# Latent attention of a hybrid decoder layer: scores two units ahead of their transposes, queries and keys loaded apart from values, shorter filling steps

## The chip, the cores and the metric

The kernel runs on one core of a Trainium2 chip. The metric is the time of the whole kernel on the device, in microseconds (us). Below, PE is TensorE (matrix products and transposes), ACT is ScalarE, DVE is VectorE, POOL is GpSimd, SP is SyncE; SP and POOL also issue the kernel's loads and stores, each in the order of its own queue.

## The reference, cut to what matters

```
h = x + 0.5 * swiglu(rms_norm(x), ffn1)
proj = rms_norm(h) @ w_in          # c_q, c_kv, k_rope, sb_qkv, gates
q, k, v = latent projections of c_q and c_kv, 8 heads: 96 for q and k, 64 for v
o_mla = softmax(mask(q k^T / sqrt(96))) v          # per head, S = 1024
o_sb  = stick_breaking(sq, sk, sv)                 # per head, 8 heads of 64
g_mla, g_sb = split(sigmoid(gates))
merged = g_mla * (o_mla @ w_branch_mla) + g_sb * (o_sb @ w_branch_sb)
h = h + merged @ w_out
h = h + 0.5 * swiglu(rms_norm(h), ffn2)
h = h + sigmoid(rms_norm(h) @ w_ple_gate) * (p @ w_ple_proj)
```

All of it is float32. SEQ is 1024, D_MODEL is 1024, each SwiGLU has 2816 hidden columns.

## The kernel before

**Arithmetic.** A float32 product is made of three matmuls: each operand is split into a rounded upper part (HI) and the rest (LO), and `mm3` (L180 holds the matmul itself) adds HI·HI, HI·LO and LO·HI. The split takes a cast on ACT (L139 for weights, L210 and L261 for results) and a subtraction on POOL or DVE (L140, L211, L262).

**Order.** The order of PE's instructions is the order in which the program writes them. The order on the other engines and on the queues of SP and POOL comes out of a scheduler that simulates the program; each engine and each queue then works strictly in that order.

**Attention.** The loop near the end of the attention phase runs over `units`, triples (m, head, un). m is 0 for stick-breaking and 1 for the latent attention (MLA). The queries of a head come in four chunks of 256 (two tiles of 128 each), and chunk c sees 256·(c+1) keys. Unit un = 0 holds chunks 0 and 1, unit 1 chunk 2, unit 2 chunk 3; in steps of 256 keys that makes 3, 3 and 4 steps, ten for a head. One step writes, in this order:

- transposes of a block of the probabilities (`tr`, L184: 3 or 4 matmuls of 128 columns into a bank `T`; ACT casts the bank to `pt` HI at L210, DVE makes LO at L211);
- the scores of a later unit, as far as `todo` has them (`A<-hd`; 128 queries against all their keys into a tile `A`, of which there are two, then the mask);
- the product of the block that was transposed two steps before with the values (`accum`, `T<-pt,hv`, 4 matmuls of 256 or 128 columns), and at the end of a chunk copies on ACT (L1124, L1129), an addition on DVE (L1130) and a split on ACT and POOL into `oT` (L1137, L1138);
- matmuls that belong to other work, up to the time `goal` of the program's own count (`fill`). During MLA this work is the output branch of stick-breaking, `branches_sb`: 192 matmuls of 512 columns in all, which show as `T<-oT,D`. Its results go over ACT (`bt`, L824), POOL (L825) and SP to the DRAM tensor `msb_d` (L826).

The softmax of an MLA tile is a maximum on DVE (L1200), an exponential on ACT (L1202), a reciprocal and a scaling on DVE (L1203, L1204); the result (`p` for chunks 0 and 1, a tile `D` of the weights' pool for chunks 2 and 3) is what a later step transposes.

Loads of a head come from POOL's queue into 9 tiles with the tag `hd`: queries HI and LO, keys HI and LO, values (`hv`).

**After attention.** `merge_up` makes the gated sum of both branches, one column tile `ct` of 128 at a time: 24 matmuls on `oT` (`T<-oT,D`), a multiplication by the gate and an addition of `msb` on DVE, and a split into `hid`. Two column tiles share one load of gates and one of `msb_d`: into `D` tiles for ct 0 and 1, into `gm` tiles for each later pair. The `gm` tiles are taken from the pool `u` and so from the memory of `o_t[1]`, the stick-breaking outputs that `branches_sb` reads. With two column tiles at hand `down_chunk` adds their product with `w_out` to h (`T<-D,hid`, 96 matmuls); for this the stream is read again from `h_spill` into `h2`, in memory that attention gives back, and two rows of `w_out` are loaded and split per chunk (the first two are called dw0 and dw1 below, tiles D_12961 and D_12966). PE writes ct 0, 1 and 2 ahead of the first down chunk (72 matmuls). All these loads are in SP's queue.

Of the kernel before, what the change touches and what calls it, by code (L numbers as in the profile page):

```python
# [27 lines left out]
H = 8  # L28
# [18 lines left out]
def hybrid_layer_kernel(  # L47
# [73 lines left out]
    v_d = dram.tile([H, S, P], F32, name="v_d")  # L121
# [579 lines left out]
    for c in range(2):  # L701
        col = slice(c * 512, (c + 1) * 512)
        for t in range(NT):
# [7 lines left out]
            n = c * NT + t  # L711
# [68 lines left out]
    def branch_w(w, ct):  # L780
        d = load_split([(0, w[:, ct * P:(ct + 1) * P].rearrange("(k q) c -> q k c", q=P))], 512)
        return d[:, :, :512].rearrange("q l (k c) -> q l k c", k=4)
# [26 lines left out]
    def branches_sb(first):  # L809

        nxt = first
        for ct in range(KT):
            d = nxt
            if ct + 1 < KT:
                nxt = branch_w(w_branch_sb, ct + 1)
            gt = load_row(gate_d, KT + ct)
            bt = rawp.tile([P, 1024], F32, tag="raw", name="bt")
            for half in range(2):
                tk = slice(half * 512, (half + 1) * 512)
                ps = bank()  # L820
                for k in range(4):
                    mm3(ps, d[:, HI, k], d[:, LO, k], o_t[1][HI][:, k, tk], o_t[1][LO][:, k, tk], k == 0, k == 3)
                    yield
                nc.scalar.copy(bt[:, tk], ps)  # L824
                nc.gpsimd.tensor_mul(bt[:, tk], bt[:, tk], gt[:, tk])  # L825
            nc.sync.dma_start(out=msb_d[ct], in_=bt)  # L826
# [6 lines left out]
    def fill(ns):  # L833
        t0 = pe["t"]
        while pe["t"] < t0 + ns:
            if next(filler[0], filler) is filler:
                break
        left[0] -= pe["t"] - t0
# [297 lines left out]
    def split_o(dst, pair, op, cs):  # L1136
        nc.scalar.copy(dst[HI][:, pair, cs], op[:, cs])  # L1137
        nc.gpsimd.tensor_sub(dst[LO][:, pair, cs], op[:, cs], dst[HI][:, pair, cs].bitcast(F32))  # L1138
# [7 lines left out]
    def load_rows(src):  # L1146
        r = ap.tile([P, S], F32R, tag="hd", name="hd", bufs=9)
        for p0, rows in src:
            nc.gpsimd.dma_start(out=r[p0:p0 + rows.shape[0]], in_=rows)
        return r  # L1150

    def load_v(src, head):
        vt = ap.tile([P, NT, P], F32R, tag="hd", name="hv", bufs=9)
        nc.gpsimd.dma_start(out=vt, in_=src[head].rearrange("(k q) c -> q k c", q=P))
        return vt
# [26 lines left out]
        return be  # L1182

    def mla_load(head):
        q = [load_rows([(0, q_d[head, :, l, :])]) for l in range(2)]
        k = [load_rows([(0, k_d[head, :, l, :])]) for l in range(2)]
        return q, k, None, load_v(v_d, head)

    def mla_products(hd, i, ps):
        q, k, _, _ = hd  # L1190
# [18 lines left out]
    units = [(m, hd, un) for m in range(2) for hd in range(H) for un in range(3)]  # L1209
# [3 lines left out]
    def head_of(m, hd):  # L1213
        if (m, hd) not in loaded and hd < H:
            loaded[m, hd] = (mla_load if m else sb_load)(hd)
        return loaded.get((m, hd))

    def scores(m, hd, idx):

        ch = idx[0] // 2  # L1220
        if (m, hd, ch) not in shared:
            shared[m, hd, ch] = [ptile(256 * (ch + 1)) for _ in range(2 - m)]
        one = acc_tile() if ch < 2 else None
        pss = [one[:, 512 * (i % 2):512 * (i % 2) + 512] if ch < 2 else acc_tile() for i in idx]
        for i, ps in zip(idx, pss):
            (mla_products if m else sb_products)(head_of(m, hd), i, ps)
        for i, ps in zip(idx, pss):
            probs[m, hd, i] = (mla_probs if m else sb_probs)(i, ps, shared[m, hd, ch])

    def start_mla():  # L1230
        first = branch_w(w_branch_sb, 0)
        fill(1e9)
        for b in range(2):
            o_t.append([upool.tile([P, 4, S], F32R, tag="u", name="oT") for _ in range(2)])
        for j in range(4):
            split_o(o_t[1], j, pairs[j], slice(0, S))
        filler[0] = branches_sb(first)
        left[0] = KT * 24 * 216.0
# [4 lines left out]
        scores(0, 0, (2 * c, 2 * c + 1))  # L1243
    fill(5500.0)
    queue = []

    def run_av():
        pt, ac = queue.pop(0)
        ac(pt)

    for n, (m, hd, un) in enumerate(units):
        if (m, hd, un) == (1, 0, 0):
            while queue:
                run_av()
            start_mla()
        todo = []
        if n + 1 < len(units):
            m2, hd2, un2 = units[n + 1]
            todo = []
            for c in unit_ch[un2]:  # L1260
                both = (2 * c, 2 * c + 1)
                todo += [(m2, hd2, ix) for ix in ([both] if m2 or c < 2 else [both[:1], both[1:]])]
        if un == 1:
            head_of(m, hd + 1) if hd + 1 < H else head_of(m + 1, 0) if m == 0 else None
        steps = []
        for c in unit_ch[un]:
            steps += av_steps(hd, c, [probs.pop((m, hd, 2 * c + a)) for a in range(2)], head_of(m, hd)[3], m == 1)
        for k, (tr, ac) in enumerate(steps):
            t0 = pe["t"]
            take = -(-len(todo) // (len(steps) - k))  # L1270
            pt = tr()
            for x_ in todo[:take]:
                scores(*x_)
            todo = todo[take:]
            queue.append((pt, ac))
            if len(queue) > 2:
                run_av()
            goal = (2500.0, 1600.0)[m]
            if m == 0 or left[0] > 0 or (hd == H - 1 and un > 0):
                fill(t0 + goal - pe["t"])  # L1280
    while queue:
# [146 lines left out]
```

## Time and profile before

| | us |
|---|---|
| time, median of 3 runs | 2365.31 (2364.64 to 2365.52) |
| the profiled execution, own time | 2360.41 |
| its span in the profile | 2358.3 |
| PE busy | 2292.8 (97%) |
| DVE, ACT, POOL busy | 1543.9, 980.4, 751.1 |
| granted TensorE clock, mean over the span | 0.991 of full speed |

The span runs from the first to the last instruction of one execution; that execution's own time is 2.1 us more than its span and 4.9 us less than the median of the runs. MLA runs from 1277.5 us (first score maximum of its first head) to 1470.9 us (first matmul of the merge).

### The profile page before, as it was taken

To read this page: it belongs to the slowest core of one execution; us is meant where nothing else is said; L and a number is where in the kernel's file an instruction comes from. 1 tells how busy PE (TensorE), PEld (TensorE's weight loads), DVE (VectorE), ACT (ScalarE), POOL (GpSimd) and SP (SyncE) were. 2 spreads that over 40 slices of the span, in tenths; PEclk is the share of its full clock that TensorE was granted. 3 is DMA by queue.
4 is the path that set the end of the run, shared out by engine and by line. 5 is a ranking of instruction groups with operands and counts; after the bars stand their busy time and mean duration, and the time that the engine had idled before them with its cause. 6 is when DMAs were issued, how large, how long until landed. Compare 5 with 4: busy or idle time off the path is not lost.

```text
span 2358.3 us, 30117 instructions
## 1 busy us (share of the span) xinstructions
PE 2292.8 (97%) x11160; PEld 1914.3 (81%) x11160; DVE 1543.9 (65%) x2026; ACT 980.4 (42%) x1676; POOL 751.1 (32%) x534
## 2 busy tenths in 40 slices
PE   8899999999999999999998998998999999999999
PEld 7788888878888998777777887887888888888887
DVE  7667676657772325668778778557766666577842
ACT  5323333325352234556666667224322333244441
POOL 6544444400031231311102332547444444300030
PEclk9999999999999999999999999999999999999999
DMA  6223233395564334984533656522333332575432
GB/s 232 85 89 112 90 121 98 108 340 176 180 188 140 89 92 116 243 215 99 126 97 87 178 146 199 187 72 72 103 112 104 97 112 90 211 281 188 141 131 80
DMA packets 293890, 331.85 MB, mean 141 GB/s; under 512 B 16624, under 2 KB 200176, under 8 KB 293744
## 3 DMA queue, kind: packets, MB, share of 16 engines
q1 hardware_dynamic: 269808, 296.38, 39.0%
q0 software_dynamic: 23936, 33.56, 6.8%
q8 instruction: 87, 1.43, 0.2%
q14 instruction: 59, 0.48, 0.1%
HBM read 230.79 MB, written 99.09 MB: 140 GB/s over the span
## 4 chain that ended last, share of the span: by engine, by line
PE 83%; DVE 6%; DMA 4%; ACT 3%; issue 2%; POOL 2%; SPq 0%; ACTq 0%; DVEq 0%; POOLq 0%
PE T L180 40%; PE T L408 34%; PE A L180 5%; PE T L184 4%; DMA raw<-in_ffn_w_out_dram 1%; DVE D L1180 1%; DMA k_d<-ev 1%; POOL D L140 1%; POOL D L369 0%; DMA v_d<-vt 0%; DMA raw<-in_ffn_w_in_dram 0%; POOL hid L262 0%; DVE pt L211 0%; DVE mx L1200 0%; DMA hs_d<-u 0%
## 5 line engine op out<-in xcount | busy, mean ns | idle before, releaser
L408 PE MATMUL T<-u,D 128*128 128x512 f32 x3168 | 735.8, 392 | 11.8 <-DVE u L431 6.6
L408 PEld LDWEIGHTS T<-u,D 128*128 128x128 f32 x3168 | 597.1, 189 | 138.7 <-DVE u L431 5.7
L180 PE MATMUL T<-D 128*128 128x512 f32 x1944 | 450.8, 392 | 4.3 <-DVE u L211 2.3
L180 PEld LDWEIGHTS T<-D 128*128 128x128 f32 x1944 | 365.4, 189 | 81.1 <-DVE u L211 2.6
L369 POOL TENSOR_TENSOR D<-ts,D 128x1024 fp32r<-128x1024 f32 x88 | 215.9, 2454 | 300.5 <-ACT D L368 294.8
L180 PE MATMUL T<-u,D 128*128 128x512 f32 x1152 | 287.5, 396 | 5.4 <-DVE ev L1008 2.5
L180 PEld LDWEIGHTS T<-u,D 128*128 128x128 f32 x1152 | 210.8, 189 | 46.3 <-DVE ev L1008 2.7
L534 ACT CAST D<-raw 128x512 fp32r<-128x512 f32 (+1 forms) x154 | 123.8, 808 | 220.5 <-PE T L180 112.5
L368 ACT CAST D<-ts 128x1024 fp32r<-128x1024 f32 x88 | 92.6, 1053 | 293.8 <-PE T L408 273.6
L180 PE MATMUL T<-D,u 128*128 128x512 f32 (+2 forms) x960 | 195.9, 362 | 0.0
L200 POOL TENSOR_SCALAR r<-ss 128x1 f32<-128x1 f32 (+2 forms) x52 | 16.6, 320 | 549.3 <-ACT un L220 401.5
L180 PEld LDWEIGHTS T<-D,u 128*128 128x128 f32 x960 | 166.2, 188 | 21.9
L535 DVE TENSOR_TENSOR D<-raw,D 128x512 fp32r<-128x512 f32 (+1 forms) x146 | 131.2, 901 | 59.3 <-ACT D L534 58.0
L211 DVE TENSOR_TENSOR pt<-T,pt 128x512 fp32r<-128x512 f32 (+1 forms) x160 | 101.0, 634 | 60.4 <-ACT pt L210 59.7
L140 POOL TENSOR_TENSOR D<-raw,D 128x1024 fp32r<-128x1024 f32 (+4 forms) x43 | 91.3, 2131 | 140.7 <-ACT D L139 140.3
L369 POOL TENSOR_TENSOR D<-raw,D 128x1024 fp32r<-128x1024 f32 x44 | 120.7, 2743 | 32.5 <-ACT D L368 32.5
L408 PE MATMUL T<-u,wb 128*128 128x512 f32 x528 | 126.8, 389 | 0.0
L385 DVE TENSOR_TENSOR ts<-raw 128x512 f32<-128x512 f32 x44 | 37.0, 841 | 133.4 <-POOL D L369 128.8
L210 ACT CAST pt<-T 128x512 fp32r<-128x512 f32 (+1 forms) x160 | 86.4, 543 | 80.4 <-PE T L184 79.7
L408 PEld LDWEIGHTS T<-u,wb 128*128 128x128 f32 x528 | 99.1, 188 | 20.6
L451 DVE TENSOR_TENSOR hidf<-u,sg 128x512 f32<-128x512 f32 x44 | 105.5, 2398 | 9.7 <-ACT sg L449 9.2
L180 PE MATMUL T<-pt,hv 128*128 128x256 f32 (+1 forms) x600 | 105.0, 298 | 6.4 <-DVE pt L211 5.4
(229 smaller groups left out, 3362.6 us busy)
## 6 DMA issues: line engine op xcount, KB each, us to landing
raw<-in_ffn_w_in_dram SPq DMA_DIRECT2D x88, 512.0 KB, 3.8
raw<-hs_d SPq DMA_DIRECT2D x154, 256.0 KB, 2.7
hs_d<-hidf SPq DMA_DIRECT2D x110, 256.0 KB, 2.3
raw<-in_ffn_w_out_dram SPq DMA_DIRECT2D x110, 256.0 KB, 3.0
raw<-in_w_in_dram SPq DMA_DIRECT2D x28, 512.0 KB, 4.4
raw<-in_ffn_w_out_dram SPq DMA_DIRECT2D x22, 512.0 KB, 6.1
h_spill<-h SPq DMA_DIRECT2D x16, 512.0 KB, 3.1
gate_d<-gate SPq DMA_DIRECT2D x16, 512.0 KB, 4.2
```

The lines of the kernel that those rows point to most:

```text
L140: low[0].tensor_sub(d[:, LO, :n], raw[:, :n], d[:, HI, :n].bitcast(F32))
L180: nc.tensor.matmul(ps, lhs, rhs, start=start, stop=stop)
L184: nc.tensor.transpose(ps, src, ident)
L210: nc.scalar.copy(hi, ps)
L211: nc.vector.tensor_sub(lo, ps, hi.bitcast(F32))
L368: nc.scalar.copy(d[:, HI], src)
L369: nc.gpsimd.tensor_sub(d[:, LO], src, d[:, HI].bitcast(F32))
L385: nc.vector.tensor_sub(ts[:, 0], b12, b11)
L408: nc.tensor.matmul(ps, b[:, l, k], a[:, r, k], start=start and k == n == 0, stop=k == 3 and n == 2, skip_group_check=True)
L451: nc.vector.tensor_mul(t["hid"][:, 512:], u3, sg)
L534: nc.scalar.copy(d[:, HI, cols], src)
L535: eng.tensor_sub(d[:, LO, cols], src, d[:, HI, cols].bitcast(F32))
```

## The change

Four things change in the attention phase.

- `mla_load` loads queries and keys only. The values of a head are loaded by `mla_values`, called in unit 1 of the head before. Queries and keys of a head are loaded in unit 2 two heads before.
- A counter `issued` replaces "the unit after this one": in MLA the scores of units up to n + 2 are written during unit n, in stick-breaking up to n + 1 as before.
- The filling goal of an MLA step is 1500 in place of 1600 of the program's nanoseconds.
- Loads of the first two MLA heads are called in unit (1, 0, 0).

```diff
     def mla_load(head):
         q = [load_rows([(0, q_d[head, :, l, :])]) for l in range(2)]
         k = [load_rows([(0, k_d[head, :, l, :])]) for l in range(2)]
-        return q, k, None, load_v(v_d, head)
+        return [q, k, None, None]
+
+    def mla_values(head):
+        hd = head_of(1, head)
+        if hd is not None and hd[3] is None:
+            hd[3] = load_v(v_d, head)
...
+    issued = 0
...
         todo = []
-        if n + 1 < len(units):
-            m2, hd2, un2 = units[n + 1]
-            todo = []
+        while issued < min(n + 1 + m, len(units) - 1):
+            issued += 1
+            m2, hd2, un2 = units[issued]
             for c in unit_ch[un2]:
                 both = (2 * c, 2 * c + 1)
                 todo += [(m2, hd2, ix) for ix in ([both] if m2 or c < 2 else [both[:1], both[1:]])]
-        if un == 1:
-            head_of(m, hd + 1) if hd + 1 < H else head_of(m + 1, 0) if m == 0 else None
+        if m == 0 and un == 1:
+            head_of(*((0, hd + 1) if hd + 1 < H else (1, 0)))
+        elif m == 1 and un == 1:
+            mla_values(hd + 1)
+        if (m, hd, un) == (1, 0, 0):
+            mla_values(0)
+            head_of(1, 1)
+        elif m == 1 and un == 2:
+            head_of(1, hd + 2)
...
-            goal = (2500.0, 1600.0)[m]
+            goal = (2500.0, 1500.0)[m]
```

**PE, first two steps with filling in a head.** `A<-hd` and `A<-mask_mla,identb` are scores and their mask, `T<-ident,p` transposes, `T<-pt,hv` the product with the values, `T<-oT,D` the filling. Unit 0 of an MLA head before, from the second score tile of its first step:

```order
L180 MATMUL A<-hd 128x256 x3
L180 LDWEIGHTS identb
L180 MATMUL A<-mask_mla,identb 128x128
L180 MATMUL T<-pt,hv 128x256 x4
L184 MATMUL T<-ident,p_10837 128x128 x4
L180 MATMUL T<-pt,hv 128x256 x2
L180 MATMUL T<-pt,hv 128x128 x2
L180 MATMUL T<-oT,D 128x512 x6
L184 MATMUL T<-ident,p_10837 128x128 x3
L180 MATMUL T<-pt,hv 128x256 x2
L180 MATMUL T<-pt,hv 128x128 x2
L180 MATMUL T<-oT,D 128x512 x6
```

and after, from the same place:

```order
L180 MATMUL A<-hd 128x512 x6
L180 LDWEIGHTS identb
L180 MATMUL A<-mask_mla,identb 128x128
L180 MATMUL T<-pt,hv 128x256 x4
L184 MATMUL T<-ident,p_10776 128x128 x4
L180 MATMUL T<-pt,hv 128x256 x2
L180 MATMUL T<-pt,hv 128x128 x2
L180 MATMUL T<-oT,D 128x512 x3
L184 MATMUL T<-ident,p_10776 128x128 x3
L180 MATMUL T<-pt,hv 128x256 x2
L180 MATMUL T<-pt,hv 128x128 x2
L180 MATMUL T<-oT,D 128x512 x6
```

The scores written in the first step are those of chunk 3 (512 + 512 columns) in place of chunk 2 (512 + 256), and the first of the two fillings has 3 matmuls in place of 6. Over the ten steps of a head the filling is 36 matmuls before (six times 6) and 27 after (3, 6, 6, 3, 3, 6).

**PE, where the filling ends.** Before, the last filling stands in unit 0 of head 5, followed by 27 steps without any:

```order
L180 MATMUL T<-oT,D 128x512 x6
L184 MATMUL T<-ident,p_12049 128x128 x3
L180 MATMUL T<-pt,hv 128x256 x2
L180 MATMUL T<-pt,hv 128x128 x2
L180 MATMUL T<-oT,D 128x512 x6
L184 MATMUL T<-ident,D 128x128 x4
L180 MATMUL A<-hd 128x512 x3
L180 MATMUL A<-hd 128x384 x3
L180 LDWEIGHTS identb
```

After, it stands in unit 0 of head 7, behind the last score of all, and seven steps with neither scores nor filling follow, up to the merge:

```order
L184 MATMUL T<-ident,p_12498 128x128 x4
L180 MATMUL T<-pt,hv 128x256 x2
L180 MATMUL T<-pt,hv 128x128 x2
L180 MATMUL T<-oT,D 128x512 x3
L184 MATMUL T<-ident,p_12498 128x128 x3
L180 MATMUL T<-pt,hv 128x256 x2
L180 MATMUL T<-pt,hv 128x128 x2
L180 MATMUL T<-oT,D 128x512 x3
L184 MATMUL T<-ident,D 128x128 x4
L180 MATMUL T<-pt,hv 128x256 x4
L184 MATMUL T<-ident,D 128x128 x4
```

The last filling has moved from head 5 to head 7.

**SP, the loads around the end of attention.** `gm`, `D<-gate_d` and `D<-msb_d` are the merge's gates and `msb` (1 MB each), `msb_d<-bt` stores the last result of the filling, `in_w_out_dram` are rows of `w_out` (the first of them in this queue is dw0, the second dw1). Before:

```order
L1306 DMA gm<-gate_d 128x2x1024
L1306 DMA gm<-msb_d 128x2x1024
L1306 DMA gm<-gate_d 128x2x1024
L1306 DMA gm<-msb_d 128x2x1024
L826 DMA msb_d<-bt 128x1024
L137 DMA raw<-in_w_branch_mla_dram 128x4x128 x2
L1306 DMA D<-gate_d 128x2x1024
L1306 DMA D<-msb_d 128x2x1024
L137 DMA raw<-in_w_out_dram 128x1024 x2
L137 DMA raw<-in_w_branch_mla_dram 128x4x128 x2
L1295 DMA h_12855<-h_spill 128x1024 x8
L206 DMA gbc<-in_ffn_norm_dram 128x1024
```

After:

```order
L1321 DMA gm<-gate_d 128x2x1024
L1321 DMA gm<-msb_d 128x2x1024
L1321 DMA D<-gate_d 128x2x1024
L1321 DMA D<-msb_d 128x2x1024
L1321 DMA gm<-gate_d 128x2x1024
L826 DMA msb_d<-bt 128x1024
L137 DMA raw<-in_w_branch_mla_dram 128x4x128
L1321 DMA gm<-msb_d 128x2x1024
L137 DMA raw<-in_w_out_dram 128x1024
L1310 DMA h_12855<-h_spill 128x1024 x8
L206 DMA gbc<-in_ffn_norm_dram 128x1024
L137 DMA raw<-in_w_out_dram 128x1024
```

The eight gate and `msb` loads stand in another order among themselves and behind the last loads for branches; dw1 stood ahead of the eight loads of h and now stands behind them and behind `gbc`.

## Rows read from the trace of the kernel before

**Rows 1.** The page: PE's busy time, and the chain that ended last by engine.

```profile
PE 2292.8 (97%) x11160; PEld 1914.3 (81%) x11160; DVE 1543.9 (65%) x2026; ACT 980.4 (42%) x1676; POOL 751.1 (32%) x534
...
PE 83%; DVE 6%; DMA 4%; ACT 3%; issue 2%; POOL 2%; SPq 0%; ACTq 0%; DVEq 0%; POOLq 0%
```

**Rows 2.** Windows of MLA heads 2 and 6, from first maximum to first maximum.

```profile
core 0: us, PE busy (x) PEld busy (x) DVE busy (x) ACT busy (x) POOL busy (x), PEclk, DMA share, GB/s
...
1328.40:1353.30 24.90, 24.73 (x158) 21.07 (x157) 19.12 (x42) 17.30 (x41) 8.56 (x11) 1.00 0.66 165
...
1426.00:1446.40 20.40, 17.19 (x121) 14.52 (x120) 17.78 (x40) 14.78 (x36) 2.96 (x4) 1.00 1.15 276
```

**Rows 3.** Stretches from the last filling to the merge, same columns.

```profile
1417.00:1436.00 19.00, 16.08 (x112) 13.54 (x111) 15.40 (x33) 13.08 (x32) 6.12 (x8) 1.00 1.07 323
1436.00:1456.00 20.00, 17.46 (x126) 15.03 (x126) 17.77 (x41) 14.83 (x37) 2.22 (x3) 1.00 0.75 193
1456.00:1471.00 15.00, 11.74 (x85) 10.06 (x84) 11.90 (x20) 12.94 (x28) 6.12 (x6) 1.00 0.29 88
```

**Rows 4.** PE's waits, 1417 to 1471 us: us in total, times, longest.

```profile
PE T L184 <- DVE D L1204: 2.6, 3, 1.3
PE T L184 <- DVE pt L211: 2.5, 3, 1.5
```

**Rows 5.** PE's timeline, last steps of attention and merge.

```profile
1466.61 0.60 PE L184 MATMUL T<-ident,D 128*128 128x128 f32 x4
...
1467.45 0.62 PE L184 MATMUL T<-ident,D 128*128 128x128 f32 x4
...
1470.88 16.57 PE L180 MATMUL T<-oT,D 128*128 128x512 f32 x72
1487.28 4.92 PE L180 MATMUL T<-D,hid 128*128 128x512 f32 x21
```

**Rows 6.** ACT by group, 1456 to 1475 us: busy us, mean ns.

```profile
L210 ACT CAST pt<-T 128x512 fp32r<-128x512 f32 x6 | 3.5, 586 | 0.6 <-PE T L184 0.6
L1129 ACT COPY op<-T 64x256 f32<-64x256 f32 x5 | 1.8, 368 | 0.1
...
L1137 ACT CAST oT<-op 128x256 fp32r<-128x256 f32 x4 | 1.6, 407 | 2.4 <-DVE op L1130 2.4
```

**Rows 7.** SP's queue, 1416 to 1486 us.

```profile
1416.91 0.37 SPq L1306 DMA_DIRECT2D gm<-gate_d  x1
...
1463.94 1.57 SPq L137 DMA_DIRECT2D raw<-in_w_out_dram  x2
...
1475.02 3.87 SPq L1295 DMA_DIRECT2D h<-h_spill  x8
1478.92 0.54 SPq L206 DMA_DIRECT2D gbc<-in_ffn_norm_dram  x1
1480.40 4.99 SPq L137 DMA_DIRECT2D raw<-in_w_out_dram  x2
```

**Rows 8.** ACT and POOL, the splits of rows of `w_out`.

```profile
1477.78 2.59 POOL L140 TENSOR_TENSOR D<-raw,D 128x1024 fp32r<-128x1024 f32 x1 [0.21 <-ACT D L139]
...
1491.22 1.05 ACT L139 CAST D<-raw 128x1024 fp32r<-128x1024 f32 x1 [0.79 <-DMA raw<-in_w_out_dram]
```

**Rows 9.** Windows of the loads of h, columns of rows 2.

```profile
1484.00:1486.00 2.00, 2.00 (x11) 1.65 (x10) 1.14 (x2) 0.54 (x1) 2.00 (x2) 1.00 1.05 424
1488.00:1490.00 2.00, 2.00 (x10) 1.65 (x9) 1.95 (x3) 0.19 (x1) 1.23 (x1) 1.00 0.98 344
```

**Rows 10.** PE's stop at the second SwiGLU's start, and windows behind it.

```profile
1622.86 2.05 PE L184 MATMUL T<-ident,s 128*128 128x128 f32 x8 [10.24 <-DVE u L211]
...
1623.00:1627.50 4.50, 4.50 (x15) 3.67 (x16) 3.99 (x7) 4.48 (x8) 4.45 (x4) 0.50 0.01 3
1628.00:1632.00 4.00, 4.00 (x27) 3.50 (x26) 0.83 (x2) 2.88 (x6) 3.84 (x4) 1.00 0.77 228
```

**Rows 11.** Loads of heads, 1300 to 1400 us: count, KB, us to landing.

```profile
hd<-k_d POOLq DMA_DIRECT2D x8, 384.0 KB, 6.5
```

## Prediction

> **What bounds the kernel now.** I began with the page: PE is busy for 97% of the span and holds 83% of the chain that ended last [rows 1], so a change here counts only by what it does to PE's idle time. Windows cut at the first score maximum of each MLA head come next. While the filling lasts, a head takes 24.9 us and PE is idle for 0.17 of it; after it, head 6 takes 20.4 us and PE is idle for 3.21 [rows 2]. From 1417 us to the merge three windows give 2.92 + 2.54 + 3.26 = 8.72 us of idle time [rows 3], almost the only idle time in MLA; the table of waits names its cause there, the scaling of the softmax on DVE (2.6 us) and the low halves of the transposed probabilities (2.5 us) [rows 4]. Without filling the chain scores, maximum, exponential, scaling, transpose is longer than PE's other work of one unit. Then I followed PE into the merge: 72 matmuls on `oT` run from 1470.88 us, the first down chunk from 1487.28 without a pause [rows 5]. What feeds that chunk stands in SP's queue and in the splits of `w_out` [rows 7, 8].
>
> **What the change does, part by part.**
>
> *Filling and scores.* No matmul is added. One of 512 columns takes 16.4/72 = 0.228 us [rows 5]. A head carries 27 fillings in place of 36 after the change: 24.9 - 9 × 0.228 = 22.85 us. DVE's work per head stays at 19.1 us [rows 2], 84% of that, so DVE still keeps up. 192/27 gives 7.1 heads, so that the filling covers heads 5 to 7, in which the 8.72 us were lost; and scores stand a unit further ahead of their transposes. So most of the 8.72 us goes. Three things stay:
>
> - The last seven steps have neither filling nor scores. A step is 1467.45 - 1466.61 = 0.84 us on PE [rows 5], seven and the last products 6.9 us. ACT needs in the same stretch five casts of 0.586 us, two shorter ones of about 0.48, three pairs of copies at 0.735, three `oT` casts at 0.407 [rows 6], and two casts of the filling's last results (taken as 0.586 each): 8.5 us, with start and handoffs 9.8. PE waits 2.9 us.
> - In a head's first step, chunk 3's scores follow close behind chunk 2's and find both `A` tiles taken. No row shows this. Nothing is the lower bound; the upper one, per head, is a reading of 1024 columns by DVE and ACT in turn, twice 0.586 each by the cast of 512 [rows 6], 2.3 us. I take 1.1 us once, at the start of MLA, where no slack has been built up, and 0.7 in the covered heads.
> - Loads of keys take 6.5 us to land [rows 11] and by the order of PE the tile that they need is released about 5 us of its work before the scores that read them. Between 0 and 1.5 us per head, so 0 to 10 in all, which would eat the whole gain; I take 0, since single loads among the eight lie below the median and filling stands in those 5 us.
>
> Sum: 8.7 - 2.9 - 1.1 - 0.7 = **4.0 us earlier at the merge** (bounds 0 and 8.7); the merge would start near M = 1466.9, the last filling end near M - 9.8.
>
> *What SP's queue makes of it.* This is the part that decides the sign. The `gm` tiles lie on the stick-breaking outputs that the filling reads, so their loads wait for the last filling. Before, that was at 1416.91 [rows 7], 54 us ahead of the merge; all of them, and dw0 and dw1 (1463.94), had landed by then. After, the last filling is only 9.8 us ahead of the merge, and SP's order puts behind it: six loads of 128x2x1024 words (1.05 MB each), a store of `msb_d` (0.52), a load for the branch (0.26), dw0 (0.52), eight loads of h (4.19), `gbc` (0.52) and then dw1 (0.52): 12.8 MB. While h is loaded the trace moves 344 to 424 GB/s [rows 9]; at 400 that is 32.1 us, and with 2.5 us for issue and landing dw1 is there at M - 9.8 + 34.6 = M + 24.8. Its cast (1.05) and the low half on POOL (2.59) [rows 8] with 0.2 for handoffs end at M + 28.6. PE wants the low half at the fifth matmul of the down chunk, M + 16.4 + 0.9 = M + 17.3. **PE stalls 11.3 us** where it did not wait before.
>
> Bounds: if the gates cost nothing, the eight loads of h alone stand ahead. They need attention's memory; before, they were issued at 1475.02 = M + 4.1, and the `w_out` piece behind h and `gbc` landed at 1491.22 = M + 20.3 [rows 5, 7, 8]. The splits end at M + 24.2, a stall of 6.9. With the 323 GB/s of the stretch in which the gates were loaded before [rows 3] the queue takes 39.7 us, and the stall is 18.9.
>
> The Trainium skill, "DMA: Bandwidth & Descriptors", section "Where 436 GB/s comes from", has transfers between HBM and SBUF bound by the HBM side at about 358 GB/s. The window at 1484 us shows 424 here, so the trace does not agree over a short stretch, and I go by the rows; by the page's figure the queue would take 35.8 us and the stall would be an estimated 15.0 us, a rival below.
>
> *The clock behind the stall.* The one stop of this length in the trace, 10.24 us, is followed by a window at 0.5 of the full clock and then by full clock again [rows 10]: the stretch at half speed lasted past the stop from 1622.9 to between 1627.5 and 1628, some 4.9 us, of which half is lost: 2.4 us. Bounds here 0 and 2.4. One matmul is done in the middle of the stall, so that I take half, 1.2.
>
> *Nothing:* loads of queries, keys and values are as many as before and on the same queue; the goal's 100 ns have no effect but the 27; PE's matmuls are the same number.
>
> **Sum.** -4.0 + 11.3 + 1.2 = **8.5 us slower**. Later work is a dense chain on PE, and the stop of 10.24 us [rows 10] hangs on DVE and loads that follow PE, so it shifts rather than absorbs. Against the profiled execution's 2360.41 that is 2368.9; that execution is 4.9 us below the median of the runs, so 2373.8 in their terms (the times below are in these).
>
> **The rivals.**
>
> A. *As above.* Gain 2 to 6, stall 9 to 13, clock 0 to 2.4, with not all of them at one end: +3 to +11. For it speaks that the wait for the filling and the order of SP's queue are fixed by the code; against it, that the landing rate is taken from other stretches. Chance 0.56, 2368 to 2376.
>
> B. *The stall is only that of the loads of h.* The gates are served while attention ends, the stall is 6.9 and the gain 4 to 8.7: -2 to +4, 2363.3 to 2369.3. For it: the 13.9 us from the last filling to the first load of h hold 5.6 MB at 400 GB/s, of the 7.6 MB that stand ahead of h; against it, the 2 MB that are left are 5 us. Chance 0.22.
>
> C. *Faster.* dw1 lands early enough to be split within a stall that is less than the gain. Its place is the fifth matmul of the down chunk; a landing at M + 13.5 is in time for it, and the kernel breaks even where dw1 lands later than that by just the gain. With the full 8.7 us gained and a stall below 4 that gives -4.7 to -8.7, 2356.5 to 2360.6. Against it: before, even with nothing but h ahead, the landing was at M + 20.3 [rows 7, 8]. Chance 0.09.
>
> D. *Slower than A.* The queue runs at 323 to 358 GB/s (a stall of 15 to 18.9), or keys come late by 1 us a head and score tiles wait in each head, so that nothing is gained: +11 to +17, 2376.5 to 2382.5. For it: 323 was the mean when the gates were loaded [rows 3], and the store of `msb_d` must land before the last gate load can start, a pause in the queue. Chance 0.13.
>
> That the change does not do what it says, scores that wait for a tile of `A` so that two units ahead is one, is in the gain's lower bound: the gain is then what the longer filling gives, and A holds.
>
> **How the numbers follow.** What a measurement of this kernel can tell from no change is about 0.2%, 4.7 us. Faster by more: C, and 0.01 of B, 0.10. Within: 0.20 of B and 0.08 of A, whose lower end is at +3: 0.28. Slower: the rest, 0.62. The range of 2362 to 2381 leaves out C and the upper end of D; A alone is 2368 to 2376.
>
> **What the changed profile would show.** Heads of about 22.9 us with PE idle under 0.3 us in each up to head 7; PE idle about 3 us in the last 10 before the merge; the merge about 4 us earlier; the first `gm` load issued some 10 us before the merge, not 54; the eight loads of h behind the gates; and a wait of PE of 9 to 13 us at the first down chunk, ended by POOL's low half of dw1, with half clock behind it. I am wrong if PE's first down chunk follows the 72 matmuls with a short wait (then B or C), if heads stay at 24 us with waits for `A` or for `hd` (then D's second half), or if the half clock costs more than the row shows.

## The result, and the profile after

The changed kernel takes 2378.43 us (median of 4 runs, 2376.32 to 2379.70); the kernel before, run beside it, 2364.97. The ratio is 1.0059, 95% interval 1.0041 to 1.0076: 13.5 us slower, inside the range, above the 8.5 us that the sum gave. The profiled execution took 2378.21 us.

Profiles of kernels that are the same up to MLA reach MLA at different times, so that stages are compared, not times on the clock. A wait for a gate on ACT, some 16 us ahead of MLA, is a good mark, since the changes act only behind it. PE's timeline of the kernel before:

```profile
1261.85 0.66 PE L184 MATMUL T<-ident,D 128*128 128x128 f32 x4 [0.54 <-ACT gate L806]
```

and of the changed kernel, with the merge's beginning, the waits at the first down chunk and, far behind, the stop that answers to [rows 10]:

```profile
1263.74 0.66 PE L184 MATMUL T<-ident,D 128*128 128x128 f32 x4 [0.57 <-ACT gate L806]
...
1476.17 16.56 PE L180 MATMUL T<-oT,D 128*128 128x512 f32 x72
1492.56 0.39 PE L180 MATMUL T<-D,hid 128*128 128x512 f32 x1
1493.92 0.73 PE L180 MATMUL T<-D,hid 128*128 128x512 f32 x2 [0.97 <-POOL D L140]
1502.62 0.80 PE L180 MATMUL T<-D,hid 128*128 128x512 f32 x1 [7.96 <-ACT D L139]
...
1505.04 22.93 PE L180 MATMUL T<-D,hid 128*128 128x512 f32 x92 [1.63 <-POOL D L140]
...
1641.69 2.04 PE L184 MATMUL T<-ident,s 128*128 128x128 f32 x8 [10.23 <-DVE u L211]
```

From mark to merge it was 1470.88 - 1261.85 = 209.03 us [rows 5], and is 1476.17 - 1263.74 = 212.43: 3.40 more, where 4.0 less was forecast. From the merge to the beginning of the stop it was 141.74 [rows 5, 10], and is 1641.69 - 10.23 - 1476.17 = 155.29: 13.55 more. These two are 17.0 us; the profiled executions lie 17.8 apart, the medians 13.5 with an interval of about 10 to 18. Each stage is read from one profiled execution, and that of before lies 4.6 us below its median; this spread seems to lie elsewhere, since e4 below has 208.82 and 141.76 in an execution of 2366.37 us.

**The merge.** SP's queue answers to [rows 7]:

```profile
1466.44 0.37 SPq L1321 DMA_DIRECT2D gm<-gate_d  x1
...
1470.57 4.43 SPq L1321 DMA_DIRECT2D gm<-msb_d  x1
1475.10 2.24 SPq L137 DMA_DIRECT2D raw<-in_w_out_dram  x1
1478.90 10.35 SPq L1310 DMA_DIRECT2D h<-h_spill  x8
...
1491.44 0.33 SPq L137 DMA_DIRECT2D raw<-in_w_out_dram  x1
```

The first gate is issued 9.7 us ahead of the merge, the eight loads of h take 10.35 us to issue, dw1 goes out at 1491.44. Its cast and low half answer to [rows 8]; the chain of waits between 1476 and 1510 us shows its landing:

```profile
1479.29 12.13 DMA h<-h_spill
...
1491.44 9.98 DMA raw<-in_w_out_dram
...
1502.64 2.36 POOL D L140
...
1505.04 5.02 PE T L180 x13
```

The first of PE's three waits, 0.97 us, is for the low half of dw0 (on POOL from 1491.04 to 1493.86); the other two are for the cast and the low half of dw1. dw1 lands at 1501.42, 25.25 us behind the merge's start. While it comes the DMA engines are full (columns of [rows 2]):

```profile
1470.00:1501.42 31.42, 23.12 (x118) 18.71 (x116) 14.19 (x21) 11.12 (x22) 15.57 (x13) 0.96 1.03 400
...
1490.00:1495.00 5.00, 3.69 (x16) 2.40 (x14) 3.04 (x4) 1.83 (x3) 5.00 (x3) 1.00 1.02 415
1495.00:1500.00 5.00, 0.00 (x0) 0.00 (x0) 0.00 (x0) 0.07 (x1) 1.76 (x2) 0.86 1.02 413
1500.00:1505.00 5.00, 0.80 (x1) 0.29 (x1) 0.00 (x0) 2.08 (x3) 2.36 (x2) 0.50 0.35 108
...
1508.00:1509.00 1.00, 1.00 (x4) 0.77 (x4) 0.14 (x1) 0.33 (x1) 0.00 (x0) 0.56 0.89 254
1509.00:1510.00 1.00, 1.00 (x6) 0.82 (x5) 0.56 (x1) 0.73 (x1) 0.20 (x1) 1.00 0.84 275
```

The clock is at 1.2 GHz (0.50) from within the stall until 1508.9, 3.8 us past its end.

**Heads with filling.** The window from 1300 to 1400 us lies in covered heads (heads with filling) in every kernel. Before:

```profile
1300.00:1400.00 100.00, 99.51 (x630) 85.12 (x629) 76.10 (x160) 68.69 (x163) 34.30 (x40) 1.00 0.63 167
```

After:

```profile
1300.00:1400.00 100.00, 94.82 (x607) 79.64 (x606) 78.58 (x165) 68.03 (x164) 30.60 (x37) 1.00 0.61 150
```

PE's idle time there goes from 0.49 to 5.18 us. Two covered heads of the changed kernel, cut at the first maxima as in [rows 2]:

```profile
1348.18:1371.96 23.78, 22.86 (x149) 19.33 (x149) 18.59 (x40) 15.94 (x39) 6.11 (x8) 1.00 0.58 143
1371.96:1396.94 24.98, 23.74 (x153) 20.00 (x153) 19.68 (x40) 16.98 (x41) 9.54 (x12) 1.00 0.61 151
```

The six covered heads from 1299.50 to 1444.45 us, each with 27 fillings, take 24.16 us in the mean with PE busy for 22.96; forecast were 22.85 with PE idle under 0.3. PE's table of waits from 1264 to 1476 us, which answers to [rows 4]:

```profile
PE T L180 <- DVE pt L211: 10.8, 15, 2.5
PE T L184 <- DVE D L1181: 2.1, 1, 2.1
PE T L184 <- ACT bt L824: 1.1, 2, 0.5
```

The table of before for its stretch, 1262 to 1471 us, has among others:

```profile
PE T L180 <- DVE pt L211: 4.2, 7, 2.5
PE T L184 <- DVE D L1204: 3.0, 4, 1.3
```

The waits for scalings are gone; products (L180 into `T`) wait 6.6 us more for low halves (one wait of 2.5 us in either table stands at the end of stick-breaking). One of the new ones, PE's timeline:

```profile
1353.03 0.60 PE L184 MATMUL T<-ident,D 128*128 128x128 f32 x4
...
1356.21 0.60 PE L184 MATMUL T<-ident,D 128*128 128x128 f32 x4
...
1357.80 0.60 PE L184 MATMUL T<-ident,D 128*128 128x128 f32 x4
1359.07 0.74 PE L180 MATMUL T<-pt,hv 128*128 128x256 f32 x4 [0.66 <-DVE pt L211]
```

DVE's:

```profile
1354.63 0.68 DVE L211 TENSOR_TENSOR pt<-T,pt 128x512 fp32r<-128x512 f32 x1
1355.23 1.68 DVE L1206 TENSOR_REDUCE mx<-A 128x1 f32<-128x640 f32 x2
...
1357.26 0.56 DVE L1210 TENSOR_SCALAR D<-D,mx 128x640 f32<-128x640 f32 x1
1357.72 0.69 DVE L140 TENSOR_TENSOR D<-raw,D 128x512 fp32r<-128x512 f32 x1
1358.33 0.69 DVE L211 TENSOR_TENSOR pt<-T,pt 128x512 fp32r<-128x512 f32 x1
```

and ACT's:

```profile
1356.92 0.61 ACT L139 CAST D<-raw 128x512 fp32r<-128x512 f32 x1
1357.43 0.58 ACT L210 CAST pt<-T 128x512 fp32r<-128x512 f32 x1
```

The product of 1359.07 belongs to the transposes of 1353.03, whose low half was done at 1355.31. It waits for the one that ends at 1359.02, of the transposes of 1356.21. It is the first product of a chunk and opens a new bank; there are four `T` banks for transposes, products and filling, and a transposed block gives its bank back only when DVE has read it. Two maxima, a scaling and a weight's low half stand ahead of that reading. DVE's order is not all of it: ACT's cast of the same block stands behind a weight's cast and ends at 1358.01, so that even a free DVE would have been done only at 1358.70 (an estimate from these rows, with ACT as it is), 0.3 us sooner, where PE waits 0.66. That the bank is what is waited for is read from these rows and the order of tiles, not tried by itself.

### The profile page after: what moved, and what is told of

It is laid out like the page before. It is cut to its first block, busy times and chain, and to the rows that moved or that the text cites. A ratio compares the mean times of both kernels' runs of the same rounds, so it can differ in the third digit from the quotient of the medians.

```text
span 2376.4 us, 30124 instructions
## 1 busy us (share of the span) xinstructions
PE 2297.6 (97%) x11160; PEld 1915.7 (81%) x11160; DVE 1541.7 (65%) x2026; ACT 978.9 (41%) x1676; POOL 750.4 (32%) x534
## 4 chain that ended last, share of the span: by engine, by line
PE 82%; DVE 5%; DMA 5%; ACT 3%; POOL 3%; issue 2%; SPq 0%; ACTq 0%; DVEq 0%; POOLq 0%
PE T L180 40%; PE T L408 34%; PE A L180 5%; PE T L184 3%; DMA raw<-in_ffn_w_out_dram 1%; DMA k_d<-ev 1%; DMA hd<-sbk_d 1%; DVE mx L1206 1%; POOL D L369 1%; POOL D L140 1%; DVE pt L211 1%; DMA h<-h_spill 1%; POOL hid L262 0%; DMA raw<-in_w_out_dram 0%; DVE u L211 0%
## 5 line engine op out<-in xcount | busy, mean ns | idle before, releaser
L180 PE MATMUL T<-D 128*128 128x512 f32 x1944 | 450.5, 392 | 5.6 <-ACT D L534 2.7
L180 PEld LDWEIGHTS T<-D 128*128 128x128 f32 x1944 | 365.2, 189 | 81.9 <-ACT D L534 3.1
L180 PE MATMUL T<-u,D 128*128 128x512 f32 x1152 | 286.0, 395 | 5.5 <-DVE ev L1008 2.6
L180 PEld LDWEIGHTS T<-u,D 128*128 128x128 f32 x1152 | 209.6, 188 | 46.1 <-DVE ev L1008 2.9
L180 PE MATMUL T<-D,u 128*128 128x512 f32 (+2 forms) x960 | 195.9, 362 | 0.0
L180 PEld LDWEIGHTS T<-D,u 128*128 128x128 f32 x960 | 166.2, 188 | 21.9
L140 POOL TENSOR_TENSOR D<-raw,D 128x1024 fp32r<-128x1024 f32 (+4 forms) x43 | 90.8, 2120 | 152.0 <-ACT D L139 151.7
L180 PE MATMUL T<-pt,hv 128*128 128x256 f32 (+1 forms) x600 | 105.7, 299 | 13.3 <-DVE pt L211 12.0
```

The costliest lines, as they stand in the source:

```text
L140: low[0].tensor_sub(d[:, LO, :n], raw[:, :n], d[:, HI, :n].bitcast(F32))
L180: nc.tensor.matmul(ps, lhs, rhs, start=start, stop=stop)
```

## The experiments

Twelve kernels ran, in groups; each is timed beside the kernel before on its own chip (medians of before: 2362.10, 2361.58, 2363.91 and 2363.72 us), so the ratio compares. Columns: ratio with its interval; us from mark to merge; us from merge to the stop; PE's idle time between 1300 and 1400 us. The last three are from one profiled execution of each kernel, which lies between 6.6 us below its median (e7) and 2.9 above (e13).

| kernel | median us | ratio | mark to merge | merge to stop | idle |
|---|---|---|---|---|---|
| before | 2364.97 | 1 | 209.03 | 141.74 | 0.49 |
| changed | 2378.43 | 1.0059 (1.0041 to 1.0076) | 212.43 | 155.29 | 5.18 |
| e1 goal 1500 alone | 2366.62 | 1.0018 (1.0009 to 1.0027) | 213.01 | 141.81 | 4.74 |
| e2 changed, goal 1600 | 2364.66 | 1.0011 (1.0002 to 1.0019) | 213.78 | 141.78 | 1.53 |
| e3 filling ends sooner | 2363.10 | 1.0008 (0.9997 to 1.0018) | 210.50 | 142.08 | 5.11 |
| e4 loads apart alone | 2364.73 | 1.0008 (0.9998 to 1.0018) | 208.82 | 141.76 | 0.66 |
| e7 later product | 2385.75 | 1.0108 (1.0088 to 1.0127) | 217.13 | 155.73 | 6.78 |
| e9 e3, less on DVE | 2365.94 | 1.0016 (1.0006 to 1.0027) | 211.04 | 142.20 | 3.65 |
| e10 e1, later product | 2368.53 | 1.0026 (1.0015 to 1.0037) | 213.99 | 141.79 | 4.49 |
| e11 e1, less on DVE | 2375.95 | 1.0049 (1.0030 to 1.0068) | 221.94 | 141.79 | 8.15 |
| e12 e2, key tiles | 2363.71 | 0.9996 (0.9987 to 1.0005) | 208.53 | 141.81 | 0.87 |
| e13 e12, later product | 2361.45 | 0.9990 (0.9981 to 0.9999) | 207.85 | 141.82 | 1.14 |
| e14 e3, key tiles, later product | 2356.21 | 0.9972 (0.9962 to 0.9982) | 202.29 | 142.77 | 1.08 |
| e15 e3, key tiles | 2364.62 | 1.0004 (0.9995 to 1.0013) | 211.05 | 143.83 | 5.08 |

**e1, one number of the change in the kernel before.**

```diff
-            goal = (2500.0, 1600.0)[m]
+            goal = (2500.0, 1500.0)[m]
```

> The kernel before with one number changed: the filling goal 1500 in place of 1600. Theory: the loss sits in two places, late low halves of the transposed probabilities on DVE (some 7 us more than forecast in MLA) and dw1 landing late at the merge (10.6 us of waits and 2.9 of half clock); the second needs the filling to last until seven steps before the merge and SP to load h ahead of dw1. Here the filling ends at the end of head 6, ten steps ahead, with dw1 ahead of h in SP's queue: no wait over 1 us at the first down chunk, the merge 0 to 4 us earlier than before, time 2361 to 2366. Rival (shorter fillings alone make it slower): the loss of 13 us appears here, 2373 or more.

No wait at the first down chunk, as the theory had it, but no gain ahead of it either: 4.0 us more to the merge. PE waits 4.74 us in the covered window with scores only one unit ahead. So the waits there come with the 27 fillings.

**e2, the change without the shorter filling.**

```diff
-            goal = (2500.0, 1500.0)[m]
+            goal = (2500.0, 1600.0)[m]
```

> The changed kernel with the goal back at 1600: scores two units ahead and loads apart, 36 fillings a head. Theory: the filling ends in head 5 again, the gates are loaded some 45 us before the merge, no wait at the first down chunk, and what is left is what two units ahead do to heads 6 and 7 without filling: between -4 and +3 us of before, 2361 to 2368. Rival (two units ahead make it slower by themselves, through score tiles or late key loads): 2370 or more, with waits of A or of hd in the covered heads.

Within the theory's range. Two units ahead alone leave 1.53 us idle in the covered window. In the heads without filling one key load is late while the gates are loaded; PE's timeline:

```profile
1444.58 0.69 PE L180 MATMUL A<-hd 96*128 96x128 f32 x2 [3.86 <-DMA hd<-k_d]
```

The windows of 10 us from 1446 and from 1466 us lie at 0.76 and 0.83 of the full clock.

**e3, the last fillings a head earlier.**

```diff
-            goal = (2500.0, 1500.0)[m]
+            goal = (2500.0, 1500.0 if hd < 6 else 1600.0)[m]
```

> The changed kernel with the goal 1600 for heads 6 and 7 alone, so that the last 9 to 12 of the 192 fillings move up into head 6 and the last one stands about ten steps before the merge in place of seven; dw1 then stands ahead of h in SP's queue. Theory (dw1 is late because 12.8 MB stand ahead of it behind the last filling): 8.4 MB stand ahead of it, it lands about 10 us after the merge's start, no wait over 1 us at the first down chunk, 11 to 14 us less than the changed kernel: 2365 to 2368. Rival (the wait comes from the order of the splits on ACT and POOL, or 10 MB around the merge are too much either way): a wait of 5 us or more stays, 2372 or more.

The stall is gone, and with it 13.2 us from the merge to the stop, as the theory had it. SP's queue of e3, whose merge starts at 1472.61:

```profile
1456.48 0.37 SPq L1321 DMA_DIRECT2D gm<-gate_d  x1
...
1474.39 0.34 SPq L137 DMA_DIRECT2D raw<-in_w_out_dram  x1
...
1476.53 1.81 SPq L1310 DMA_DIRECT2D h<-h_spill  x4
```

The first gate goes out 16.1 us ahead of the merge in place of 9.7 (the pair into `D` tiles only at its start, 1472.18), and dw1 ahead of h in place of behind it. Both moved, so e3 does not say how much each did.

**e4, the loads alone.**

```diff
-        while issued < min(n + 1 + m, len(units) - 1):
+        while issued < min(n + 1, len(units) - 1):
...
-            goal = (2500.0, 1500.0)[m]
+            goal = (2500.0, 1600.0)[m]
```

> The kernel before with the loads alone changed: queries and keys two heads ahead in unit 2, values apart, scores one unit ahead, goal 1600. Theory: it costs nothing by itself, within 1.5 us of before: 2361 to 2364. Rival (the loads apart collide with the filling's or take tiles from the keys): waits of PE for hd, 2365 or more.

No difference: both stages are those of before.

**e7, the product a step later in the changed kernel.**

```diff
-            if len(queue) > 2:
+            if len(queue) > 2 + m:
...
-            pt = ap.tile([P, 2, 512], F32R, tag="pt", name="pt", bufs=4)
+            pt = ap.tile([P, 2, 512], F32R, tag="pt", name="pt", bufs=5)
...
-        r = ap.tile([P, S], F32R, tag="hd", name="hd", bufs=9)
+        r = ap.tile([P, S], F32R, tag="hd", name="hd", bufs=8)
```

> The changed kernel with the product with the values three steps behind its transposes in place of two in MLA (five pt tiles in place of four, eight tiles for loads of heads in place of nine to make room). Theory (the low halves come late because DVE does maxima and scalings of other score tiles first): PE's waits for pt in MLA, 10.8 us, fall below 4, the merge starts 5 to 8 us earlier, the wait for dw1 stays at 9 to 13 us: 2370 to 2374. Rival (DVE has too much work per head altogether): the waits move to the score tiles or the transposes, the merge is not earlier: 2377 to 2380. Late loads through the eighth tile would show as waits of PE for hd.

The waits for low halves fall, but the eighth tile makes keys late. PE's waits from 1255 to 1640 us:

```profile
PE A L180 <- DMA hd<-k_d: 8.9, 9, 2.1
PE T L180 <- ACT D L139: 7.8, 2, 6.2
PE T L180 <- DVE pt L211: 4.0, 5, 2.5
```

The run is spoiled for its question; e10 and e14 ask it again.

**e10, e9 and e11, the low halves in other ways.** e10 is e1 with the diff of e7. e9 is e3, and e11 is e1, with two things moved to POOL:

```diff
-            nc.vector.tensor_add(op[mine, cs], op[mine, cs], tmp[mine])
+            (nc.gpsimd if mla else nc.vector).tensor_add(op[mine, cs], op[mine, cs], tmp[mine])
...
     def start_mla():
+        low[0] = nc.gpsimd
```

> The kernel of e1 (before with goal 1500) with the product with the values three steps behind its transposes, five pt tiles, eight tiles for loads of heads. It asks the question of e7 again where scores are only one unit ahead, so that keys are not short of tiles. Theory (DVE's order makes the low halves late by under a step): waits for pt in the covered heads fall from about 5.5 us to under 1.5, the time by 3 to 5 from e1: 2361 to 2364. Rival (keys and values need the ninth tile here too): waits for hd of 3 us or more, the time at e1's 2366.6 or above.

> The kernel of e3 with two things moved from DVE to POOL in MLA: the addition of a head's output (0.42 us, some four a head) and the low halves of the filling's weights (0.69 us, one or two a head). Theory (low halves of the transposed probabilities come late because they stand in DVE's order behind other work, a weight's low half among it): PE's waits for pt between 1300 and 1450 us fall from 5 to 6 us to under 3, and the time by 2 to 4: 2359 to 2361 where the kernel before has 2362. Rival (the waits come from the cast on ACT or the transposes, not from DVE's queue): the waits stay at 5 to 6 us, the time within 1 us of e3.

> The kernel of e1 with the two things moved from DVE to POOL as in e9. Theory: as there, waits for pt from 5.5 us to under 3, the time 2 to 4 below e1: 2362.5 to 2364.5. Rival: no difference from e1's 2366.6.

All three missed. In e10 waits for low halves almost vanish, and with scores one unit ahead the wait comes back at the scalings, PE's waits from 1286 to 1478 us:

```profile
PE T L184 <- DVE D L1204: 5.0, 5, 1.6
PE T L184 <- ACT op L1129: 2.3, 5, 0.9
```

e9's idle time falls from 5.11 to 3.65 us in the window, but copies and the last heads give it back. e11 needs 8.9 us more than e1 to the merge; a hold-up of DVE beside POOL, told at the end, has a part in it, but how large a part is not shown.

**e12, key tiles.** e2 with the low half of the keys in tiles of their own:

```diff
-        k = [load_rows([(0, k_d[head, :, l, :])]) for l in range(2)]
+        k = [load_rows([(0, k_d[head, :, 0, :])]), None]
+        if head:
+            k[1] = ap.tile([P, S], F32R, tag="op", name="kl", bufs=4)
+            nc.gpsimd.dma_start(out=k[1][:QK], in_=k_d[head, :, 1, :])
+        else:
+            k[1] = load_rows([(0, k_d[head, :, 1, :])])
```

> The kernel of e2 (changed kernel, goal 1600) with the low half of the keys of heads 1 to 7 loaded into the four tiles that hold pairs of outputs (tag op) in place of the nine tiles of heads, so that no key waits for a tile. Theory (two units ahead halve the waits of the heads without filling, and e2 lost this to one late key load, 3.86 us, and the half clock behind it, some 4): both vanish, the stretch from the last wait for the gate before MLA to the merge falls from 213.8 us to 205 to 207 where before has 209.0, the time 2 to 4 below before: 2357.5 to 2360 if before is at 2361.6. Rival (the key is late because the gates' loads share the DMA engines, whatever tile it has): a wait for a key of 3 us or more stays, 2363 or more.

The late key is gone and 5.2 us with it, so it was the tile that made it late. The rest of the expectation missed: 208.53 us to the merge, not 205 to 207, and no measurable difference to before. A stretch at half clock remains in the last head (0.83 in the mean from 1460 to 1470 us).

**e13, e14, e15.** e13 is e12 with the diff of e7; e14 is e3 with both; e15 is e14 without the diff of e7.

> The kernel of e12 with the product with the values three steps behind its transposes (five pt tiles, eight tiles of heads). Theory after e10 (DVE and ACT have little slack per head, a wait that is taken from the low halves comes back at the scalings and the copies): within 1.5 us of e12. Rival (the low halves were the limit, e10 was spoiled by something else): 2 to 4 us below e12, with waits for pt under 1 us and no more waits for D.

> The kernel of e3 (27 fillings a head, the last ones moved up into head 6) with the key tiles of e12 and the later product of e13, so that neither a late key nor a wait for pt is left that a step more could hide. Theory (what 27 fillings a head cost is DVE's and ACT's work per head and no single order): waits in the covered heads stay above 4 us, the time within 2 us of e3, 0 to 2 above before: 2361 to 2364. Rival (the order of the low halves was all of it): waits in the covered heads under 2.5 us, the merge 4 us earlier than in e3: 2357 to 2360.

> The kernel of e14 without the later product: the kernel of e3 with the key tiles of e12 alone, so that e14's gain is told apart between its two edits. Theory (what 27 fillings a head cost are low halves of the transposed probabilities that are late by under a step, which only the later product hides; the keys were not waited for in e3): waits for pt in the covered heads stay at 5 to 6.6 us, the time within 2 us of e3, 0 to 2 above before. Rival (the key tiles are what e14 gains by): the waits fall under 3 us and the time lies 4 to 7 below before.

e13 does not decide between theory and rival: it lies 2.3 us below e12 by the medians, 1.4 by the ratios, and takes 0.7 us less to the merge. e14 broke the theory that I had formed after e10: it is faster than both kernels, by 0.28% of before. Its covered window:

```profile
1300.00:1400.00 100.00, 98.92 (x640) 84.52 (x640) 83.11 (x175) 72.04 (x173) 31.92 (x38) 1.00 0.65 162
```

DVE is busier there than in any other run, 83.11 us of 100, and PE idle only 1.08. e15 tells that the later product is what does it: without it idle time is 5.08 and the time that of before.

## Why the prediction was right about the sign, and where its sum failed

**The merge's stall: right, and nearly in size.** Forecast were dw1 at 24.8 us behind the merge's start and a stall of 11.3; measured are 25.25, and 0.97 + 7.96 + 1.63 = 10.56 in the waits. The bounds were 6.9, for the loads of h alone, and 18.9; it lies between. In the chain of waits h is released by attention's end and dw1 by h's place in the queue, while the gates in flight stretch what lies between: from the first load of h to the landing of the piece of `w_out` behind them it took 1491.22 - 1475.02 = 16.2 us before [rows 7, 8], and 1501.42 - 1478.90 = 22.5 now. e3 shows the whole: with the filling's end 6.4 us earlier and dw1 ahead of h, 13.2 of the 13.55 us go. The 34.6 us of the sum came out as 34.98, from the first gate's issue at 1466.44 to the landing, and its 400 GB/s as 400 from 1470.00 us to the landing, with 413 to 415 in the windows of the stall. By the figure of the Trainium skill, "DMA: Bandwidth & Descriptors", section "Where 436 GB/s comes from", of about 358 GB/s on the HBM side, the stall would have been an estimated 15.0 us; these windows do not agree with it.

**The clock: mis-sized, within its bounds.** The sum took 1.2 us, between 0 and 2.4. Measured are 13.55 - 10.56 = 2.99 us of stage beyond the waits. Half of the 3.8 us behind the stall, 1.9, is the half clock; the rest is in the table of waits, which counts from a matmul's modelled end. By starts, 1493.92 to 1502.62 is 8.70 us for two matmuls of 0.23, so 8.2 lost where 7.96 stands; the other two waits come to 1.1 and 2.2 in this way. That is 11.6 us in all, where 11.3 were forecast, and with the 1.9 the 13.5 of the stage.

**The gain ahead of the merge: wrong.** The step that failed is "DVE's work per head stays at 19.1 us [rows 2], 84% of that, so DVE still keeps up", and with it the 0.7 us for the covered heads. The work itself was as forecast, 18.9 us on DVE and 22.96 on PE per covered head; but PE idles 1.2 us in each, so that a head gets 0.7 us shorter in place of 2.05. In place of -4.0 us the stage grew by 3.4. Of these, 0.9 lie between the mark and the last wait at MLA's start, a stretch that takes 22.6 to 23.8 us in all these runs, whatever the change, by how long the clock stays at half speed in it (a mean of 0.86 of the full clock over the 24 us behind the mark before, 0.79 now). The other 2.5 lie behind that wait, in the heads. By waits of at least 0.14 us they cost 6.6 us from 24 us behind the mark to the old end of the filling (155 us behind it), where before has 1.1; the heads behind that cost 3.7, where before has 8.7. So the longer filling did what was forecast at the end (2.9 expected there; the 8.7 were 4.5 for scalings, 2.7 for low halves and 1.5 for ACT), and gave it back ahead of it. Net, these waits grew by 0.5 us; the other 2.0 of the 2.5 stand in no wait of the tables, and no run says where they lie. e1 and e2 part the two causes: 27 fillings with scores one ahead wait 4.74 us in the covered window, 36 fillings with scores two ahead 1.53. Shorter filling steps bring a first product sooner behind the transposes of the step before, and four banks and the orders of DVE and ACT leave no slack there, as far as the rows above show it. e14 shows that DVE's load as such was no obstacle: at 83% busy it keeps up when the product comes a step later. For that the scores have to be two units ahead, otherwise the scalings are late (e10), and the keys need a tile (e7); this is read from the waits of these two, which differ from e14 in more than the one thing. With 36 fillings a head the same two settings give only 0.1% (e13).

**The loads:** right; e4 costs nothing, and in the changed kernel PE waited for no `hd` tile. **The `A` tiles:** forecast 1.1 us at the start of MLA, measured 0.6 and 0.3 (waits for ACT's exponential, L1208). **The stop behind:** it shifted and absorbed nothing, 10.23 us for 10.24 [rows 10].

By its time it was D (2376.5 to 2382.5, chance 0.13), just above A: the stall of A, with the half of D that says nothing is gained, though not through late keys and hardly through score tiles. So the sign came from the stall, and the sum was short by 5 us on the median because the gain was counted on a share of busy time. What stays open: how the stall divides between the gates ahead and h ahead of dw1, where the 2.0 us without a wait lie, and whether the waiting product in the covered heads is held by its bank alone.

## What to carry to other kernels

An engine that is 80% busy can still be late for the one wait that matters: look at what stands ahead of the awaited instruction in its order, and how many steps lie between. Work that fills gaps also holds memory; before it is made to last longer, list which loads wait for its last instruction and what stands behind them in their queue. Settings that only pay together (scores further ahead, product a step later, shorter filling steps, as in e14) look next to useless in the runs that lack one of them (e2, e10, e13).

## What the runs showed of the hardware that was not expected

DVE was held up beside POOL. In e11 a scaling of 128x896, 0.69 us elsewhere, took 2.90, three times, each ending behind a low half on POOL that started after it. DVE's timeline:

```profile
1300.83 2.90 DVE L1204 TENSOR_SCALAR D<-D,mx 128x896 f32<-128x896 f32 x1
1303.66 0.68 DVE L211 TENSOR_TENSOR pt<-T,pt 128x512 fp32r<-128x512 f32 x1
```

and POOL's:

```profile
1300.42 1.03 POOL L1149 DMA_DIRECT2D hd<-q_d  x2
1301.44 0.51 POOL L1149 DMA_DIRECT2D hd<-k_d  x1
1301.96 1.28 POOL L140 TENSOR_TENSOR D<-raw,D 128x512 fp32r<-128x512 f32 x1
```

The scaling begins while POOL issues loads and ends at 1303.7, 0.5 us behind the end of L140. The Trainium skill, "SBUF — State Buffer", section "Who interferes with whom", has GpSimd share DVE's second pair of ports as an exclusive lock, so that of two instructions that want this pair one blocks for the other's whole length; the rows agree as to the blocking, and show 2.2 us of it over several POOL instructions in a row. That the ports are its cause was not tried here. e9 has one such scaling, 2.57 us at 1296.37. Moving work from a busy DVE to an idle POOL is therefore not free.
